# A running log-sum-exp: partition totals in a float32r tile of their own, one-pass matmuls, and the running sum kept in PSUM for three of four chunks

## The chip, the cores and the metric

The kernel runs on one core of a Trainium2 chip. The metric is the device time of one execution in microseconds (us). Every job here timed the kernel before on the same chip in the same rounds. A verdict of faster or slower takes a difference of more than 2%. Ratios are the mean time of one kernel's runs over the mean time of the other's runs of the same rounds, so they are not quite the ratio of the medians quoted beside them.

## The reference

```python
B, S, D = (4, 4096, 4128)                     # x: float32, standard normal
out[:, 0, :] = x[:, 0, :]
for t in range(1, S):                         # logaddexp along S
    mx = np.maximum(out[:, t-1, :], x[:, t, :])
    out[:, t, :] = mx + np.log(np.exp(out[:, t-1, :] - mx) + np.exp(x[:, t, :] - mx))
```

The inputs are small enough to leave the maximum out: the result is the logarithm of a running sum of exponentials along S. 271 MB are read and 271 MB written.

## The kernel before

A step takes 384 rows (256 in four of the 44 steps); each of the 128 partitions holds three (two) consecutive rows of 4128 columns. A step is cut into four chunks of 1024 columns; 32 columns are left over, the tail. Per chunk:

- ScalarE: Exp in place.
- VectorE, `own`: add row 0 to row 1 and row 1 to row 2, so that the last row holds the partition's total.
- TensorE, `head`: a strictly triangular matrix (`excl`) times the totals adds the sum of all partitions above, in PSUM, to the running sum that is there.
- VectorE, `add_above`: add PSUM to all three rows.
- TensorE, `pick`: copy the last row of the last partition, the new running sum, into PSUM for the next step.
- ScalarE: Ln in place; after the fourth chunk the step is stored.

```python
bufs = 4
above = [psum.tile([P, CH], FP32, name=f"above{c}") for c in range(n_main)]   # all of PSUM
above_t = above[last][:, CH - MM:CH - MM + tail]
# ... cut ...
    def own(self):
        x = self.t.xt
        for j in range(1, self.t.r):
            v = x[:, j, self.a:self.b]
            add(v, x[:, j - 1, self.a:self.b], v)
    def head(self):
        for s in range(0, CH, MM):
            mm(above[self.c][:, s:s + MM], excl, t.xt[:, t.r - 1, a + s:a + s + MM],
               start=t.first, stop=True)
    def add_above(self):
        v = t.xt[:, :, a:a + CH]
        add(v, v, above[self.c].unsqueeze(1).to_broadcast([P, t.r, CH]))
    def pick(self, s0=0, s1=CH):
        # ... cut: for each bank
                mm(above[self.c][:, s:s + MM], pick, t.xt[:, t.r - 1, a + s:a + s + MM], start=True)
# ... cut ...
ahead = bufs - 1
for s in steps[:ahead]:
    s.load()
# ... cut: in result(k), after Ln of the last chunk of a step ...
            k.t.store()
            if stored + ahead < len(steps):
                steps[stored + ahead].load()
# ... cut: the order of work, one chunk per turn ...
for g, k in enumerate(chunks):
    chunks[g + 1].own(); chunks[g + 1].head()
    chunks[g + 2].act(ACT.Exp)
    finish(chunks[g - 1]); result(chunks[g - 1])      # tail; Ln, store
    k.add_above(); k.pick()
```

Loads and stores are issued from one queue in this order, and each engine works its instructions in order. Ln of a chunk stands behind Exp of the chunk three places later on ScalarE, and `pick` and `head` read rows that Ln then overwrites.

The softmax here doesn't subtract the row's maximum and nothing guards it: scores larger than these inputs give would overflow.

## Time and profile before

| | before |
|---|---|
| time, median of 3 (range) | 1265.17 us (1264.26 to 1267.58) |
| profiled run | 1268.05 us, span 1266.3 us |
| moved by DMA | 541 MB, 427 GB/s over the span |
| busy: DMA queue / VectorE / ScalarE / TensorE | 99.3% / 77% / 73% / 60% |

The page gives the busy share of each engine, and one line per group of like instructions with what ended the idle time in front of them. "DMA share" in the busy times by stretch is the mean over the 16 DMA engines. The lines themselves stand in the prediction.

One line that it does not show is from the view of who waited for whom in the kernel before (engine and line, waited for: us in total, times, longest us):

```profile
ACT xt L106 <- PE above L74: 33.9, 38, 4.2
```

In 38 of the 44 steps, ScalarE's last Ln waits for matmuls that still read the rows it will overwrite.

### The profile page before, as it was taken

The numbers are of one execution on the slowest core, as the hardware profiler recorded it, in microseconds if no ns is written. First come the engines' busy times: TensorE is split into PE (matmuls) and PEld (weight loads), VectorE is DVE, ScalarE is ACT, GpSimd is POOL, SyncE is SP. The second block draws the span as 40 slices with busy tenths as digits, with TensorE's granted clock in tenths as the row PEclk, the third lists the DMA queues.
The fourth block names the chain that finished last, engine by engine and source line by source line (L and its number), as shares of the span: only waits on it lengthen the run. The fifth ranks groups of instructions, "written<-read, shape, count | busy, mean of one in ns | idle before, by whom it ended". The sixth has DMA issues, their size and how long they took to land.

```text
span 1266.3 us, 4623 instructions
## 1 busy us (share of the span) xinstructions
PE 760.5 (60%) x1512; PEld 289.0 (23%) x1512; DVE 980.6 (77%) x597; ACT 923.8 (73%) x353; POOL 1.1 (0%) x8
## 2 busy tenths in 40 slices
PE   4676665555666666666366666665646656666562
PEld 1222222222222222222122222222212222222220
DVE  3998777777777878788579878777857978787793
ACT  4887666777777777767668777666866877766794
POOL 0000000000000000000000000000000000000000
PEclk9998888887788888888779888888877988888886
DMA  9999999999999999999999999999999999999998
GB/s 409 384 425 424 427 429 443 426 427 440 432 429 441 426 430 440 429 431 433 434 434 434 429 440 430 431 437 433 432 419 434 426 433 433 431 432 438 426 418 349
DMA packets 12695, 541.35 MB, mean 427 GB/s; under 512 B 1409, under 2 KB 1409, under 8 KB 1409
## 3 DMA queue, kind: packets, MB, share of 16 engines
q1 hardware_dynamic: 12672, 541.07, 99.3%
q8 instruction: 12, 0.20, 0.1%
q14 instruction: 11, 0.08, 0.0%
HBM read 270.53 MB, written 270.53 MB: 427 GB/s over the span
## 4 chain that ended last, share of the span: by engine, by line
DMA 67%; DVE 12%; ACT 9%; PE 8%; issue 1%; SPq 0%; ACTq 0%
DMA xt<-in_x_dram 63%; DVE xt L77 12%; ACT xt L106 9%; PE above L74 8%; DMA out_dram<-xt 5%; SPq L97 0%; ACTq L106 0%; SPq L94 0%; DVE carry_t L146 0%
## 5 line engine op out<-in xcount | busy, mean ns | idle before, releaser
L106 ACT ACTIVATE xt<-xt 128x3072 f32<-128x3072 f32 (+2 forms) x352 | 922.5, 2693 | 327.0 <-DMA xt<-in_x_dram 290.5
L74 PE MATMUL above<-xt,excl 128*128 128x512 f32 (+1 forms) x792 | 443.1, 687 | 348.7 <-DVE xt L77 339.4
L77 DVE TENSOR_TENSOR xt<-xt 128x1024 f32<-128x1024 f32 (+1 forms) x336 | 413.4, 1230 | 255.0 <-ACT xt L106 249.4
L77 DVE TENSOR_TENSOR xt<-xt,above 128x3072 f32<-128x3072 f32 (+3 forms) x220 | 582.9, 2651 | 11.7 <-PE above L74 10.3
L74 PE MATMUL above<-xt,pick 128*128 128x512 f32 x640 | 330.7, 630 | 130.0 <-DVE xt L77 130.0
L74 PEld LDWEIGHTS above<-xt,excl 128*128 128x128 f32 x792 | 162.6, 229 | 601.5 <-issue 490.5
L74 PEld LDWEIGHTS above<-xt,pick 128*128 128x128 f32 x640 | 113.6, 198 | 307.4 <-DVE xt L77 227.2
L74 PEld LDWEIGHTS above<-carry_t,pick 128*128 128x128 f32 x80 | 20.8, 271 | 51.4 <-DVE xt L77 48.2
L74 PE MATMUL above<-carry_t,pick 128*128 128x32 f32 x80 | 17.5, 308 | 10.1 <-DVE xt L77 10.1
L146 DVE COPY carry_t<-xt 32x32 f32<-32x32 f32 x40 | 7.1, 178 | 1.4
L56 ACT ACT_TABLE_LOAD x1 | 1.3, 1283 | 0.8 <-PEq L214 0.8
L69 DVE MEMSET carry_t<- 128x32 f32 x1 | 0.1, 85 | 0.9 <-PEq L214 0.9
L27 POOL TENSOR_SCALAR_AFFINE_SELECT pick<-pick 128x128 f32<-128x128 f32 x1 | 0.3, 293 | 0.0
L21 POOL TENSOR_SCALAR_AFFINE_SELECT excl<-excl 128x128 f32<-128x128 f32 x1 | 0.3, 292 | 0.0
L19 POOL MEMSET excl<- 128x128 f32 x1 | 0.2, 204 | 0.3 <-POOLq L214 0.3
L26 POOL MEMSET pick<- 128x128 f32 x1 | 0.2, 204 | 0.0
L214 POOL MEMSET const-bfloat16-1.0<- 128x1 bf16 x1 | 0.1, 101 | 0.0
L214 POOL MEMSET const-uint8-127<- 128x1 uint8 x1 | 0.1, 101 | 0.0
L214 POOL MEMSET const-float32-0.0<- 128x1 f32 x1 | 0.1, 98 | 0.3 <-issue 0.3
L214 POOL MEMSET const-float32-1.0<- 128x1 f32 x1 | 0.1, 98 | 0.0
## 6 DMA issues: line engine op xcount, KB each, us to landing
xt<-in_x_dram SPq DMA_DIRECT2D x40, 6192.0 KB, 41.1
out_dram<-xt SPq DMA_DIRECT2D x40, 6192.0 KB, 27.0
xt<-in_x_dram SPq DMA_DIRECT2D x4, 4128.0 KB, 36.2
out_dram<-xt SPq DMA_DIRECT2D x4, 4128.0 KB, 19.6
```

Of the source, the lines that this page charges most:

```text
L19: nc.gpsimd.memset(excl, 1.0)
L21: nc.gpsimd.affine_select(out=excl, in_=excl, pattern=[[1, P]], compare_op=mybir.AluOpType.is_ge, fill=0.0, base=-1, channel_multiplier=-1,)
L26: nc.gpsimd.memset(pick, 0.0)
L27: nc.gpsimd.affine_select(out=pick, in_=pick, pattern=[[0, P]], compare_op=mybir.AluOpType.not_equal, fill=1.0, base=-(P - 1), channel_mul ...
L56: nc.scalar.preload_act_table_set("natural_log_exp_and_others")
L69: nc.vector.memset(carry_t, 0.0)
L74: nc.tensor.matmul(pt, lhsT=w, rhs=rhs, start=start, stop=stop, skip_group_check=True)
L77: nc.vector.tensor_tensor(out=o, in0=a, in1=b, op=mybir.AluOpType.add)
L106: nc.scalar.activation(v, v, func)
L146: nc.vector.tensor_copy(carry_t[96:, :], t.xt[96:, t.r - 1, t0:D])
L214: nc = _bacc.Bacc("TRN2", target_bir_lowering=False, num_devices=1)
```

## The change

Its intent: a fp32 matmul takes several passes through the array; with the totals in a tile of type float32r it takes one. The tile also frees Ln from waiting for matmuls. The running sum is completed in PSUM by a second triangular matrix, `rest` (`excl` + `rest` = all ones), which the three chunks kept there get in one pass. The last chunk shares its PSUM with the tail, so these two cannot keep their running sum there; they pass it from step to step through a fp32 copy of the last row (`carry`) and a fp32 `pick`. (The aim seems to be that the rounding of float32r does not add up over the steps.) VectorE pays: the last row is now "total tile + PSUM", so the add of three rows becomes one of two rows and one of one row, plus the copy. Three more things came along: four loads are issued at the start instead of three, the last step is no longer pipelined into the one before it, and each step starts with the chunk that has the tail.

```diff
-            for j in range(1, self.t.r):
-                v = x[:, j, self.a:self.b]
-                add(v, x[:, j - 1, self.a:self.b], v)
+            full = tpool.tile([P, CH + tail], FP32R, name="tot")      # two buffers
+            self.tot = full[:, :self.b - self.a]
+            for j in range(1, r - 1):
+                add(self.row(j), self.row(j - 1), self.row(j))
+            add(self.tot, self.row(r - 2), self.row(r - 1))
@@ head
-                mm(above[self.c][:, s:s + MM], excl, t.xt[:, t.r - 1, a + s:a + s + MM], ...)
+                if through:                                            # last chunk
+                    mm(o, pick, carry[:, s:e], start=True)
+                mm(o, excl, self.tot[:, s:e], start=self.t.first)
@@ add_above
-            add(v, v, above[self.c].unsqueeze(1).to_broadcast([P, t.r, CH]))
+                v = t.xt[:, :n, a:b]                                   # n = r - 1
+                add(v, v, p.unsqueeze(1).to_broadcast(v.shape))
+            add(t.xt[:, n, a:b], self.tot[:, a - self.a:b - self.a], p)
+            if cr is not None and not t.final:
+                nc.vector.tensor_copy(cr[96:, :], t.xt[96:, n, a:b])
@@ pick -> complete
+            if self.c != lastc and not self.t.final:
+                for o, s, e in self.banks():
+                    mm(o, rest, self.tot[:, s:e])
@@ loads
-    for s in steps[:ahead]:
+    for s in steps[:bufs]:
         s.load()
-            if stored + ahead < len(steps):
+            if bufs <= stored + ahead < len(steps):
@@ order of work (now starting with the chunk that has the tail)
-    for g, k in enumerate(chunks):
+    for part in (steps[:-1], steps[-1:]):
+        chunks = [Chunk(s, c) for s in part for c in order]
+        for g in range(-2, N + 1):
```

More of the change, by code (lines that the diff above doesn't have):

```diff
@@ L8 @@
 FP32 = mybir.dt.float32
+FP32R = mybir.dt.float32r
 ACT = mybir.ActivationFunctionType
@@ L16, in _constants, with select @@
 def _constants(nc, pool):
-    excl = pool.tile([P, P], FP32, name="excl")
-    nc.gpsimd.memset(excl, 1.0)
-    nc.gpsimd.affine_select(
-        out=excl, in_=excl, pattern=[[1, P]], compare_op=mybir.AluOpType.is_ge,
-        fill=0.0, base=-1, channel_multiplier=-1,
-    )
-    pick = pool.tile([P, P], FP32, name="pick")
-    nc.gpsimd.memset(pick, 0.0)
-    nc.gpsimd.affine_select(
-        out=pick, in_=pick, pattern=[[0, P]], compare_op=mybir.AluOpType.not_equal,
-        fill=1.0, base=-(P - 1), channel_multiplier=1,
-    )
-    return excl, pick
+    def select(dtype, fill, op, base, step, name):
+        t = pool.tile([P, P], dtype, name=name)
+        nc.gpsimd.memset(t.bitcast(FP32), 1.0 - fill)
+        nc.gpsimd.affine_select(
+            out=t, in_=t, pattern=[[step, P]], compare_op=op, fill=fill, base=base,
+            channel_multiplier=-step if step else 1,
+        )
+        return t
+    ge, ne = mybir.AluOpType.is_ge, mybir.AluOpType.not_equal
+    return (
+        select(FP32R, 0.0, ge, -1, 1, "excl"),
+        select(FP32R, 0.0, ge, 0, -1, "rest"),
+        select(FP32, 1.0, ne, 1 - P, 0, "pick"),
+    )
 @with_exitstack
@@ L50, with mm @@
     assert S % P == 0
-    n_main = D // CH
-    tail = D - n_main * CH
-    t0 = n_main * CH
-    last = n_main - 1
+    NC = D // CH
+    tail = D - NC * CH
+    t0 = NC * CH
+    order = [NC - 1] + list(range(NC - 1))
+    firstc, lastc = order[0], order[-1]
     nc.scalar.preload_act_table_set("natural_log_exp_and_others")
     consts = ctx.enter_context(tc.tile_pool(name="consts", bufs=1))
-    excl, pick = _constants(nc, consts)
+    excl, rest, pick = _constants(nc, consts)
     bufs = 4
     xpool = ctx.enter_context(tc.tile_pool(name="xpool", bufs=bufs))
+    tpool = ctx.enter_context(tc.tile_pool(name="tpool", bufs=2))
     cpool = ctx.enter_context(tc.tile_pool(name="cpool", bufs=1))
     psum = ctx.enter_context(tc.tile_pool(name="psum", bufs=1, space=bass.MemoryType.PSUM))
-    above = [psum.tile([P, CH], FP32, name=f"above{c}") for c in range(n_main)]
-    above_t = above[last][:, CH - MM:CH - MM + tail]
+    above = [psum.tile([P, CH], FP32, name=f"above{c}") for c in range(NC)]
+    above_t = above[lastc][:, :tail]
+    carry = cpool.tile([P, CH], FP32, name="carry")
     carry_t = cpool.tile([P, tail], FP32, name="carry_t")
+    nc.vector.memset(carry, 0.0)
     nc.vector.memset(carry_t, 0.0)
     ctx.enter_context(tc.manual_schedule())
-    def mm(pt, w, rhs, start=False, stop=False):
-        nc.tensor.matmul(pt, lhsT=w, rhs=rhs, start=start, stop=stop, skip_group_check=True)
+    def mm(o, w, rhs, start=False):
+        nc.tensor.matmul(o, lhsT=w, rhs=rhs, start=start, stop=True, skip_group_check=True)
     def add(o, a, b):
@@ L101, in __init__, with row @@
             self.t, self.c = step, c
-            self.a, self.b = c * CH, D if c == last else (c + 1) * CH
+            self.a, self.b = c * CH, D if c == NC - 1 else (c + 1) * CH
+        def row(self, j):
+            return self.t.xt[:, j, self.a:self.b]
         def act(self, func):
@@ L108, in own @@
         def own(self):
-            x = self.t.xt
-            for j in range(1, self.t.r):
-                v = x[:, j, self.a:self.b]
-                add(v, x[:, j - 1, self.a:self.b], v)
-        def head(self):
-            t, a = self.t, self.a
-            for s in range(0, CH, MM):
-                mm(above[self.c][:, s:s + MM], excl, t.xt[:, t.r - 1, a + s:a + s + MM],
-                   start=t.first, stop=True)
-        def add_above(self):
-            t, a = self.t, self.a
-            v = t.xt[:, :, a:a + CH]
-            add(v, v, above[self.c].unsqueeze(1).to_broadcast([P, t.r, CH]))
@@ L127, in pick @@
-        def pick(self, s0=0, s1=CH):
-            t, a = self.t, self.a
-            if not t.final:
-                for s in range(s0, s1, MM):
-                    mm(above[self.c][:, s:s + MM], pick, t.xt[:, t.r - 1, a + s:a + s + MM],
-                       start=True)
-        def tail_head(self):
-            t = self.t
-            if not t.first:
-                mm(above_t, pick, carry_t, start=True)
-            mm(above_t, excl, t.xt[:, t.r - 1, t0:D], start=t.first, stop=True)
-        def tail_add(self):
-            t = self.t
-            v = t.xt[:, :, t0:D]
-            add(v, v, above_t.unsqueeze(1).to_broadcast([P, t.r, tail]))
-            if not t.final:
-                nc.vector.tensor_copy(carry_t[96:, :], t.xt[96:, t.r - 1, t0:D])
+            r = self.t.r
@@ new lines, in own, with banks @@
+            full = tpool.tile([P, CH + tail], FP32R, name="tot")
[3 more added lines that the diff above has]
+            add(self.tot, self.row(r - 2), self.row(r - 1))
+        def banks(self):
+            for s in range(0, CH, MM):
+                yield above[self.c][:, s:s + MM], s, s + MM
+        def head(self):
+            through = self.c == lastc and not self.t.first
+            for o, s, e in self.banks():
+                if through:
+                    mm(o, pick, carry[:, s:e], start=True)
+                mm(o, excl, self.tot[:, s:e], start=self.t.first)
@@ new lines, in tail_head, with sums @@
+        def tail_head(self):
+            if not self.t.first:
+                mm(above_t, pick, carry_t, start=True)
+            mm(above_t, excl, self.tot[:, CH:], start=self.t.first)
+        def sums(self, a, b, p, cr):
+            t = self.t
+            n = t.r - 1
+            if n:
+                v = t.xt[:, :n, a:b]
[3 more added lines that the diff above has]
+                nc.vector.tensor_copy(cr[96:, :], t.xt[96:, n, a:b])
@@ L148, with complete @@
+        def add_above(self):
+            self.sums(self.a, self.a + CH, above[self.c], carry if self.c == lastc else None)
+            if self.c == firstc:
+                self.sums(t0, D, above_t, carry_t)
+        def complete(self):
+            if self.c != lastc and not self.t.final:
+                for o, s, e in self.banks():
+                    mm(o, rest, self.tot[:, s:e])
     steps = []
@@ L153 @@
             parts.reverse()
+        assert min(parts) > 1
         row = 0
@@ L158 @@
         assert row == S
-    chunks = [Chunk(s, c) for s in steps for c in range(n_main)]
     ahead = bufs - 1
-    for s in steps[:ahead]:
+    for s in steps[:bufs]:
         s.load()
     stored = 0
-    def finish(k):
-        if k.c == last:
-            k.tail_add()
-            k.pick(CH - MM)
     def result(k):
@@ L172, in result @@
         k.act(ACT.Ln)
-        if k.c == last:
+        if k.c == lastc:
             k.t.store()
-            if stored + ahead < len(steps):
+            if bufs <= stored + ahead < len(steps):
                 steps[stored + ahead].load()
             stored += 1
-    chunks[0].act(ACT.Exp)
-    chunks[1].act(ACT.Exp)
-    chunks[0].own()
-    chunks[0].head()
-    for g, k in enumerate(chunks):
-        if g + 1 < len(chunks):
-            chunks[g + 1].own()
-            chunks[g + 1].head()
-        if g + 2 < len(chunks):
-            chunks[g + 2].act(ACT.Exp)
-        if g:
-            finish(chunks[g - 1])
-            result(chunks[g - 1])
-        k.add_above()
-        if k.c == last:
-            k.tail_head()
-            k.pick(0, CH - MM)
-        else:
-            k.pick()
-    finish(chunks[-1])
-    result(chunks[-1])
+    for part in (steps[:-1], steps[-1:]):
+        chunks = [Chunk(s, c) for s in part for c in order]
+        N = len(chunks)
+        for g in range(-2, N + 1):
+            if 0 <= g + 2 < N:
+                chunks[g + 2].act(ACT.Exp)
+            if 0 <= g + 1 < N:
+                chunks[g + 1].own()
+                chunks[g + 1].head()
+            if 0 <= g < N:
+                chunks[g].add_above()
+                if g + 1 < N and chunks[g + 1].c == firstc:
+                    chunks[g + 1].tail_head()
+                chunks[g].complete()
+            elif g == -1:
+                chunks[0].tail_head()
+            if 0 <= g - 1:
+                result(chunks[g - 1])
 _INS = ['x']
```

## The prediction

> **What bounds the kernel now.** I read the page first, then the busy times by stretch (one row per window), then the timeline at both ends, because the page says that the middle has one owner.
>
> ```profile
> PE 760.5 (60%) x1512; PEld 289.0 (23%) x1512; DVE 980.6 (77%) x597; ACT 923.8 (73%) x353; POOL 1.1 (0%) x8
> ...
> PEclk9998888887788888888779888888877988888886
> DMA  9999999999999999999999999999999999999998
> ...
> q1 hardware_dynamic: 12672, 541.07, 99.3%
> ...
> L74 PE MATMUL above<-xt,excl 128*128 128x512 f32 (+1 forms) x792 | 443.1, 687 | 348.7 <-DVE xt L77 339.4
> L74 PE MATMUL above<-xt,pick 128*128 128x512 f32 x640 | 330.7, 630 | 130.0 <-DVE xt L77 130.0
> ```
>
> No compute engine is above 77%; the DMA queue that carries loads and stores is at 99.3%. The two matmul rows are what the change attacks, but most of the idle time of TensorE in front of them is waiting for VectorE: TensorE is a follower here. The busy times by stretch (columns: window, its length, busy time and number of instructions of PE, PEld, DVE, ACT, POOL, then TensorE clock, DMA share, GB/s) tell where the transfers are not saturated:
>
> ```profile
> 41.00:44.00 3.00, 2.11 (x5) 0.84 (x6) 2.97 (x4) 3.00 (x2) 0.00 (x0) 1.00 0.42 176
> 68.00:70.00 2.00, 1.03 (x3) 0.19 (x1) 2.00 (x1) 2.00 (x2) 0.00 (x0) 1.00 0.94 396
> 100.00:1200.00 1100.00, 666.59 (x1318) 253.00 (x1318) 861.17 (x522) 806.80 (x304) 0.00 (x0) 0.87 1.00 432
> 1234.00:1240.00 6.00, 4.50 (x11) 1.64 (x10) 5.68 (x5) 6.00 (x4) 0.00 (x0) 1.00 0.21 91
> ```
>
> For 1100 us the share is 1.00 at 432 GB/s. The idle time of the transfers is all at the ends: 3 x 0.58 = 1.7 us at 41 us, 2 x 0.06 = 0.1 us at 69 us, 6 x 0.79 = 4.7 us at 1234 us, together 6.5 us, half a per cent of the span. The bytes do not change (541 MB; 541.07 MB at 432 GB/s are 1252 us), so nothing that the change does can win more than these 6.5 us unless the rate itself moves. That decides the verdict; the rest of this text is about the sign of a few microseconds.
>
> **What the Trainium skill says.** (1) "DMA: Bandwidth & Descriptors", Specifications, gives a fabric ceiling of 435 GB/s; the trace agrees, 432 in the long window. So the middle has no reserve. (2) "FP8 and Floating Point Precision", TensorE Precision Notes: true fp32 takes four passes through the array. The trace: an fp32 matmul of 512 columns is two records, which start 0.43 us apart at full clock (the timeline from 23.97 to 25.26 us), so one pass is estimated at 0.21 us. (3) "TensorE: Matmul & The Clock Gate", Part 1: the clock halves when the array idles. The trace agrees: four records take 3.39 us at 1242.92 us, where the granted clock is 0.5. TensorE with less work will be cold more often. (4) "VectorE: DVE Perf Modes", The TRN2 errata: a fp32 tensor_tensor costs (N+151)/0.96 ns. The trace: 128x3072 takes 3348 ns, 128x2048 2282, 128x1024 1222; the formula gives 3357, 2291, 1224. So cutting one add in two costs about 0.15 us.
>
> **The change part by part.** A step is 384 rows (256 in four of the 44), a chunk a quarter of its columns.
>
> *TensorE.* Before, a step has 16 fp32 matmuls of 512 columns (8 excl, 8 pick), 32 records x 0.43 = 13.7 us warm, plus the tail's small ones; the page has 760.5/44 = 17.3 us. After: 8 excl and 6 rest in one pass, 14 x 0.21 = 3.0 us; two fp32 pick matmuls for the last chunk, 4 x 0.43 = 1.7; the tail's 0.6. That is 5.3 us warm, 233 us for 44 steps, and some 300 to 350 us at a colder clock: 410 to 460 us of TensorE work go. All of it lies beside saturated transfers, worth 0 us in the middle.
>
> *VectorE.* The row sums stay (the last goes to the new tile instead of in place). The add from PSUM is cut in two: 2.28 + 1.22 = 3.50 instead of 3.35, four times a step: +0.6 us. The tail's add in two: +0.2. A copy of 32x1024 into the carry: if it runs at two elements a cycle, 0.7 us (estimate from the same page's tier table, fp32 copy 2x). Sum 1.5 us on a step of 23.1 (the row for 1143 to 1172 us shows 23.18 busy in 29): 24.6 us, still below the 29.3 us that two transfers take. Total DVE near 1045 us. Also 0 us in the middle. A wait may appear: with two buffers, the second row sum writes the tile that the rest matmuls of the chunk before are reading, and they start only when the add before has ended; the first row sum (1.2 us) covers two passes, the weight load and a warm clock, about 0.8 us, and just misses a cold one, about 1.4.
>
> *The waits.* Before, the last Ln of a step waits for the matmuls that read its rows in place:
>
> ```profile
> 40.65 20.62 ACT L106 ACTIVATE xt<-xt 128x2112 f32<-128x2112 f32 x8 [1.24 <-PE above L74]
> 65.51 21.50 ACT L106 ACTIVATE xt<-xt 128x3168 f32<-128x3168 f32 x8 [4.25 <-PE above L74]
> ```
>
> With the separate tile nothing on TensorE reads the rows that Ln overwrites, so these go, except through the chain add, copy, Ln.
>
> *Start.* Before, load 3 is issued with store 0, at 43.03 us; the first three loads are moved by 41.3 us and the transfers stand still for 1.7 us. After, four loads are issued at once: 1.6 + 9.8 + 3 x 14.6 = 55.2 us of work (packets of 8 per engine at 1.22 and 1.83 us). Store 0 at about 42 us is in time. Store 1 was issued at 68.38; without the wait for PE I get about 64, working VectorE's queue forward from load 1's landing at 27.7 us at 5.9 us a chunk; store 0 ends at 65. Gain of the start: 1.8 us.
>
> *End.* This is the part that I could get wrong. Before:
>
> ```profile
> 1201.74 13.38 ACT L106 ACTIVATE xt<-xt 128x3072 f32<-128x3072 f32 x5 [7.35 <-DMA xt<-in_x_dram]
> 1215.73 8.23 ACT L106 ACTIVATE xt<-xt 128x3168 f32<-128x3168 f32 x3 [0.61 <-PE above L74]
> 1226.15 20.85 ACT L106 ACTIVATE xt<-xt 128x2048 f32<-128x2048 f32 x10 [2.19 <-DMA xt<-in_x_dram]
> 1249.67 1.96 ACT L106 ACTIVATE xt<-xt 128x2112 f32<-128x2112 f32 x1 [2.67 <-DVE xt L77]
> ```
>
> The last load lands at 1226; the last-but-one store goes out when its Ln is through, at 1240.2 (six activations after 1226.15), 6 us after the transfers ran dry. It takes 14.7 us, to 1254.9, and the last store (ready at 1251.7) follows on its heels for 9.8 us, to 1264.7; 1.6 us later the span ends. After, the last-but-one step is drained alone. From its landing (1201.7 - 1.8 = 1199.9): first row sums done at +5.3, the add and copy of the step before +9.4, row sums +11.7, add with tail +15.8, two chunks of 5.8 to +27.4, last add and copy +31.5, Ln 2.8 to +34.3: store at 1234.2, just as the transfers run dry (1234 - 1.8), so the 4.7 us gap shrinks to 2. But only then does ScalarE, in order, begin the last step. Its chain: Exp 1.95, row sum 1.25, wait for the second Exp, row sum to 5.1, add with tail to 7.8, row sum and add 8.95 and 11.3, 12.5 and 14.9, the last add to 17.4 (perhaps 0.5 more for the two cold fp32 matmuls), Ln 1.95: 19.6 us. Store at about 1254.0, that is 2.3 us later than before. The transfers finished the store before it at 1249 to 1251, so the new gap is some 4 us, and the end is 1254.0 + 0.5 + 9.8 + 1.6 = 1265.9, less than a microsecond below the 1266.3 of before. What separating wins for one store it loses for the next.
>
> *Sum:* start -1.8, end +1.4: about -0.4 us in the span. 1265.17 - 0.4, rounded: 1264.7 us.
>
> **The rivals.** *A: the transfers stay the bound and both ends gain* (the ends' 6.5 us all go, 1259 us). For it: the separate last step clearly aims at it. Against it: the last step then has to be computed in the 15 us that the store before takes, and I count 19.6. *B: VectorE becomes the bound.* 24.6 us a step against 29.3; even with a stall of 0.5 us on three chunks a step it is 26. For it only the copy at one element a cycle (+0.5) and a tile in float32r that adds more slowly, which I see no sign of. If it did reach 30 us a step, 1300 us and more. *C: a serial end.* The drain of both steps longer than counted, stalls of VectorE on cold matmuls (0.5 us a chunk): the span 3 to 4 us longer, 1269 us. *D: transfers hidden anyway, nothing moves*: within 1 us of 1265, which is close to my own number for a different reason.
>
> **Range and chances.** The start is worth 0 to -2, the end -5 to +4, and the three runs of before lie 3.3 us apart. So 1260 to 1269 us. Both edges are inside 2% (1240 to 1290), and only B or a changed rate leaves it: within 2% 0.97, faster 0.01, slower 0.02.
>
> **What would show it.** Right: DMA share 1.00 at 432 GB/s in the long window; PE busy falls to 300 or 350 us and the clock with it; DVE rises to about 1045 us; ScalarE no longer waits for PE before Ln; the gap at 41 us is gone; the last-but-one store is issued about 34 us after its load landed and the last one about 20 us after that, with transfers idle for some 4 us between. Wrong: DVE busy above 1150 us or long waits of DVE for PE (B); idle transfers in the middle; a last store issued before 1251 us (A). The prediction fails if VectorE's ops on the new type have another cost than the fp32 ones, or if the rate of the transfers changes with the order of loads and stores.

## The result, and the profile after

The changed kernel takes 1265.7 us (median of 4, 1264.33 to 1265.97), the kernel before 1264.72 us in the same rounds: ratio 1.0003, 95% interval 0.9984 to 1.0021. A second comparison, 5 runs against 9, is E12 below: 1.0004 (0.9992 to 1.0017). The result is correct, and the change moves nothing.

The page of the changed kernel: busy totals, TensorE clock and DMA in 40 slices, the DMA queue, and the three groups of matmuls.

```profile
PE 480.5 (38%) x876; PEld 220.3 (17%) x876; DVE 1024.4 (81%) x858; ACT 921.0 (73%) x353; POOL 1.5 (0%) x10
...
PEclk9865555565555555556556565656555656555656
DMA  9999999999999999999999999999999999999997
...
q1 hardware_dynamic: 12672, 541.07, 99.4%
...
L83 PE MATMUL above<-tot,excl 128*128 128x512 f32 (+1 forms) x396 | 255.1, 714 | 476.9 <-DVE tot L86 472.6
...
L83 PE MATMUL above<-tot,rest 128*128 128x512 f32 x240 | 129.2, 633 | 205.1 <-DVE xt L86 205.1
L83 PE MATMUL above<-carry,pick 128*128 128x512 f32 x160 | 139.5, 972 | 0.0
```

TensorE has 280 us less to do and its granted clock fell from 0.87 to 0.58; VectorE has 44 us more; the DMA queue is as full as it was. The stretches of the changed kernel, in the columns of the prediction:

```profile
41.00:44.00 3.00, 1.22 (x2) 0.50 (x2) 2.83 (x6) 3.00 (x3) 0.00 (x0) 1.00 1.22 528
100.00:1200.00 1100.00, 423.48 (x769) 193.27 (x768) 901.22 (x749) 803.71 (x306) 0.00 (x0) 0.56 1.00 433
1228.00:1233.00 5.00, 0.00 (x0) 0.00 (x0) 0.87 (x2) 4.00 (x2) 0.00 (x0) 0.50 0.67 287
1247.00:1252.00 5.00, 0.00 (x0) 0.00 (x0) 1.57 (x2) 3.23 (x2) 0.00 (x0) 0.87 0.27 116
```

(A packet counts in the stretch where it starts, so a short one can show more than 1.) The idle stretch at 41 us is gone. The one at 1234 us has become two: 5 x 0.33 = 1.7 us in front of the last store but one, 5 x 0.73 = 3.7 us in front of the last. ScalarE at the end, from its timeline:

```profile
1197.23 21.50 ACT L118 ACTIVATE xt<-xt 128x3168 f32<-128x3168 f32 x8 [7.74 <-DMA xt<-in_x_dram]
1219.08 2.76 ACT L118 ACTIVATE xt<-xt 128x3072 f32<-128x3072 f32 x1 [0.34 <-DVE xt L86]
1224.94 2.77 ACT L118 ACTIVATE xt<-xt 128x3072 f32<-128x3072 f32 x1 [3.10 <-DVE xt L86]
1229.00 10.02 ACT L118 ACTIVATE xt<-xt 128x3072 f32<-128x3072 f32 x5 [1.29 <-DVE carry L155]
...
1248.67 1.91 ACT L118 ACTIVATE xt<-xt 128x2048 f32<-128x2048 f32 x1 [0.35 <-DVE xt L86]
```

The load of the last step but one lands at 1197.2. Its last Ln is the first 2.8 us of the group at 1229.00; it ends at 1231.8, and the first Exp of the last step follows at once. The very last Ln ends at 1250.6. So the lone last step takes 18.8 us, while the store before it is moved in 14.6 (8 packets of 1.83 us on each engine).

### The profile page after: what moved, and what is told of

It reads as the page before. It is cut to its first block, busy times and chain, and to the rows that moved or that the text cites. A ratio compares the mean times of both kernels' runs of the same rounds, so it can differ in the third digit from the quotient of the medians.

```text
span 1262.5 us, 3545 instructions
## 1 busy us (share of the span) xinstructions
PE 480.5 (38%) x876; PEld 220.3 (17%) x876; DVE 1024.4 (81%) x858; ACT 921.0 (73%) x353; POOL 1.5 (0%) x10
## 3 DMA queue, kind: packets, MB, share of 16 engines
q1 hardware_dynamic: 12672, 541.07, 99.4%
## 4 chain that ended last, share of the span: by engine, by line
DMA 69%; ACT 19%; issue 7%; DVE 3%; SPq 0%; PE 0%; DVEq 0%; ACTq 0%
DMA xt<-in_x_dram 63%; ACT xt L118 19%; DMA out_dram<-xt 6%; DVE xt L86 3%; DVE tot L86 1%; SPq L106 0%; PE above L83 0%; DVE carry L155 0%; DVEq L239 0%; ACTq L118 0%; DVE carry_t L155 0%; DVEq L86 0%
## 5 line engine op out<-in xcount | busy, mean ns | idle before, releaser
L118 ACT ACTIVATE xt<-xt 128x3072 f32<-128x3072 f32 (+3 forms) x352 | 919.7, 2692 | 328.8 <-DMA xt<-in_x_dram 315.0
L83 PE MATMUL above<-tot,excl 128*128 128x512 f32 (+1 forms) x396 | 255.1, 714 | 476.9 <-DVE tot L86 472.6
L86 DVE TENSOR_TENSOR xt<-xt,above 128x2048 f32<-128x2048 f32 (+3 forms) x220 | 393.4, 1788 | 0.0
L86 DVE TENSOR_TENSOR xt<-xt 128x1024 f32<-128x1024 f32 (+1 forms) x160 | 197.0, 1231 | 179.9 <-ACT xt L118 177.5
L86 DVE TENSOR_TENSOR tot<-xt 128x1024 fp32r<-128x1024 f32 (+1 forms) x176 | 217.1, 1234 | 40.4 <-ACT xt L118 18.9
L86 DVE TENSOR_TENSOR xt<-tot,above 128x1024 f32<-128x1024 f32 (+1 forms) x220 | 221.5, 1007 | 0.0
L83 PEld LDWEIGHTS above<-tot,excl 128*128 128x128 f32 x396 | 104.4, 305 | 607.4 <-DVE tot L86 566.9
L83 PE MATMUL above<-tot,rest 128*128 128x512 f32 x240 | 129.2, 633 | 205.1 <-DVE xt L86 205.1
L83 PE MATMUL above<-carry,pick 128*128 128x512 f32 x160 | 139.5, 972 | 0.0
L83 PEld LDWEIGHTS above<-tot,rest 128*128 128x128 f32 x240 | 53.1, 276 | 295.9 <-DVE xt L86 294.1
```

Of the source, the lines that this page charges most:

```text
L83: nc.tensor.matmul(o, lhsT=w, rhs=rhs, start=start, stop=True, skip_group_check=True)
L86: nc.vector.tensor_tensor(out=o, in0=a, in1=b, op=mybir.AluOpType.add)
L118: nc.scalar.activation(v, v, func)
```

## The experiments

My theory: the DMA engines are the bound in the middle, nothing on the compute engines counts there, and only the two ends could move. The main rivals: the one-pass matmuls do pay and VectorE gives it back; or the gain waits at the ends and is lost to the order of work there.

### E1: transfers alone

All arithmetic taken out of the changed kernel; each store waits for its load. Wrong result.

```diff
-                chunks[g + 2].act(ACT.Exp)
-                chunks[g + 1].own(); chunks[g + 1].head()
-                chunks[g].add_above() ...
-        k.act(ACT.Ln)
```

> The changed kernel with all arithmetic taken out (no Exp, sums, matmuls or Ln): the same 44 loads and 44 stores, each store waiting for its load alone. The result is wrong on purpose. My theory (the transfers are the bound, about 433 GB/s, and all else lies beside them): a span of about 1257 us, the sum of the packets' time (1254.7 us in the profile of before) plus 1.6 us before and after; time 1258 to 1261 us, 0.4% below both kernels. Rival (the compute holds the transfers back in the middle, or slows their packets): clearly faster, under 1240 us, with packets shorter than 1.83 us.

Measured: 1258.34 us against 1264.17 (ratio 0.9951, 0.9938 to 0.9965), as expected. (The 1254.7 us in the expectation is close to the packet time of the changed kernel, 99.4% of 1262.5; the profile of before has 99.3% of 1266.3, 1257.4 us.) Three stretches of this run (columns: window, length, DVE, ACT and POOL busy, clock, DMA share, GB/s):

```profile
100.00:1200.00 1100.00, 0.00 (x0) 0.00 (x0) 0.00 (x0) 1.00 1.00 433
1250.00:1253.00 3.00, 0.00 (x0) 0.00 (x0) 0.00 (x0) 1.00 0.61 264
1253.00:1255.00 2.00, 0.00 (x0) 0.00 (x0) 0.00 (x0) 1.00 0.15 66
```

Without a single instruction of compute the middle runs at 433 GB/s, the rate of both kernels. That settles the middle: compute takes next to nothing from it. The last two lines held a warning that I passed over at first. There is nothing to wait for at the end of this run, and yet the share falls to 0.15 (two to three of the 16 DMA engines, on the mean) before the end: the engines do not finish together.

### E2: the kernel before, with four loads at the start

```diff
-    for s in steps[:ahead]:
+    for s in steps[:bufs]:
-            if stored + ahead < len(steps):
+            if bufs <= stored + ahead < len(steps):
```

> The kernel before with one part of the change: four loads at the start instead of three. Theory: the idle stretch of the transfers at 41 us goes (1.7 us), the end is as before: 1.5 to 2 us less, a ratio to before of about 0.9985. Rival (what is won at the start is waited for again later, because the end is set by another wait): ratio 1.000, with a longer idle stretch near 1234 us.

Measured: 1264.71 against 1264.17 us, ratio 1.0000 (0.9988 to 1.0013). The 1.7 us did not come; the rival's number is right. Its place for them was not quite: the stretch at 41 us is full, and the transfers run dry later, at 66 us, because the second store is not there yet. E10, which starts the same way, shows it at its worst. ScalarE's timelines of E2 and then of E10:

```profile
63.80 13.54 ACT L106 ACTIVATE xt<-xt 128x3168 f32<-128x3168 f32 x5 [2.55 <-PE above L74]
```

```profile
66.58 13.54 ACT L106 ACTIVATE xt<-xt 128x3168 f32<-128x3168 f32 x5 [5.19 <-PE above L74]
```

and the transfers of E10 behind it:

```profile
66.00:70.00 4.00, 4.00 (x9) 1.48 (x7) 4.00 (x2) 3.42 (x2) 0.00 (x0) 0.86 0.14 58
```

The second store hangs on that Ln, which waits 2.55 us or 5.19 us for TensorE; the store is issued at about 66.7 us in E2 and 69.5 in E10. By the packet records, four loads and the first store are done by 67.4 us in E2 and 67.8 in E10. In the changed kernel Ln does not wait for TensorE, the second store is issued at 63.8 us, and the transfers do not run dry. So the early load alone does not fill the start, Ln has to be free of TensorE as well; and E4 will show that the tile of its own is not enough either if its matmuls are slow. One thing stays open: in E2's own profiled run the late store costs only some 0.5 us, so the profile leaves 1 us or more of gain that the median of five runs does not show.

### E3: the changed kernel, with the end pipelined again

```diff
-    for part in (steps[:-1], steps[-1:]):
+    for part in (steps,):
```

> The changed kernel with its end undone: the last step is pipelined into the one before, as in the kernel before. Theory: the idle time at the end only moves back from between the last two stores to in front of the last but one; two gaps of 2.3 and 3.9 us become one of 4 to 6 us: span 1261 to 1264 us, the same as the changed kernel within 2 us. Rival A (separating the last step is worth its 4.7 us): 4 us slower than the changed kernel. Rival B (it costs): 3 us faster.

Measured: 1263.66 us, ratio to before 0.9993 (0.9980 to 1.0005), where the changed kernel has 1.0003 and 1.0004. The profile has one idle stretch at the end, 10 x 0.66 = 6.6 us from 1226 to 1236 us, and none in front of the last store. As the theory said, separating the last step only moves the idle time; it may cost 1 us, which these intervals do not resolve (the packet records, below E12, show 0.8).

### E4: the changed kernel, with its matmuls in fp32

```diff
-FP32R = mybir.dt.float32r
+FP32R = mybir.dt.float32
```

> The changed kernel with the new tile and its two constants in fp32 instead of float32r, so that its matmuls take four passes again: the part that the change is named for, undone alone. Theory (TensorE lies beside the transfers): the same as the changed kernel within 3 us, PE busy back above 750 us, VectorE waiting for TensorE in front of the row sum that writes the tile (0.5 to 1 us a chunk, 60 to 130 us in all against 11), hidden in the middle; only the end is longer by 1 to 3 us. Rival (the one-pass matmuls do pay, and the split adds of VectorE give it back): 1% or more slower than the changed kernel.

Measured: 1273.38 us, ratio to before 1.0070 (1.0057 to 1.0082). Neither expectation holds: more than my 3 us, less than the rival's 1%. Where the 8 us come from is in the waits and stretches. First the changed kernel's wait of VectorE for TensorE, then the same in E4 with three stretches of E4:

```profile
DVE tot L86 <- PE above L83: 11.4, 43, 1.4
```

```profile
DVE tot L86 <- PE above L83: 92.5, 92, 2.1
```

```profile
66.00:72.00 6.00, 2.19 (x6) 1.36 (x7) 5.90 (x6) 4.04 (x2) 0.00 (x0) 0.73 0.38 160
1233.00:1240.00 7.00, 0.59 (x2) 0.00 (x0) 2.57 (x3) 5.71 (x3) 0.00 (x0) 0.73 0.59 255
1253.00:1261.00 8.00, 2.84 (x6) 1.06 (x6) 4.57 (x4) 4.45 (x3) 0.00 (x0) 0.94 0.04 19
```

The row sum that writes the tile waits for the four-pass `rest` matmuls that read it. In the middle that is hidden. At the start the second store is late and the transfers stand for 6 x 0.62 = 3.7 us; at the end for 7 x 0.41 + 8 x 0.96 = 10.6 us, where the changed kernel has 1.7 + 3.7 = 5.4. Together 8.9 us, against some 8 us measured (0.67% of 1264). So within this arrangement the one-pass matmuls are worth about 8 us, all of it at the ends, and they pay for what the rest of the change costs there.

### E5 and E6: the compute without its transfers

The compute of both kernels on all columns, with loads and stores of only the first 1024 after the first four (full) loads. The result is wrong.

```diff
+    held = [xpool.tile([P, R, D], FP32, name=f"xt{i}") for i in range(bufs)]
-            nc.sync.dma_start(out=self.xt, in_=self.dram(x))
+            nc.sync.dma_start(out=self.xt[:, :, :CH], in_=self.dram(x)[:, :, :CH])   # first four: whole tile
-            nc.sync.dma_start(out=self.dram(out), in_=self.xt)
+            nc.sync.dma_start(out=self.dram(out)[:, :, :CH], in_=self.xt[:, :, :CH])
-            nc.scalar.activation(v, v, func)
+            nc.scalar.activation(v, v, func, scale=0.125 if func == ACT.Exp else 1.0)
```

> The kernel before with a quarter of the transfers: four full tiles are loaded once, then each step loads and stores only its first 1024 columns and computes on all; Exp has a scale of 0.125, so that the recycled values stay in range. The result is wrong on purpose. It shows how fast the compute alone goes. Theory: VectorE sets the pace, 24 to 25 us a step as in the profile of before between 43 and 93 us (stores 25.7 and 24.2 us apart), so 1070 to 1110 us. Rival (TensorE sets it): the same time, but with VectorE idle more than 15% of the middle, waiting for PE or for Ln that waits for PE.

> The changed kernel with the same quarter of the transfers (wrong on purpose as well). Theory: what the matmuls no longer cost, the split adds and the copy of the carry do cost on VectorE, so the compute alone is no faster either: 24.5 to 25.5 us a step, 1080 to 1125 us, a ratio to the run before it of 1.00 to 1.02. Rival (the change does pay, and only the transfers hide it): at least 3% faster than the kernel before with a quarter of the transfers.

Measured: 1043.44 us for the kernel before, 1079.0 us for the changed one: the change makes the compute 3.4% slower (1079.0/1043.44). The theory's numbers missed: the kernel before is quicker than I had read off its start (1070 to 1110 us), so the ratio of the two is 1.034 and not 1.00 to 1.02. The rival for E6, a change that pays once most of the transfers are gone, has the wrong sign. The busy totals, E5 and then E6:

```profile
PE 727.6 (70%) x1512; PEld 271.7 (26%) x1512; DVE 977.1 (94%) x597; ACT 919.7 (88%) x353; POOL 1.1 (0%) x8
```

```profile
PE 474.8 (44%) x876; PEld 217.6 (20%) x876; DVE 1021.3 (95%) x858; ACT 932.6 (87%) x353; POOL 1.5 (0%) x10
```

VectorE is the bound of the compute in both, at 94 and 95%. TensorE, at 70% in E5, was not it. The 44 us that the change adds to VectorE show up nearly whole, as 36 us.

### E7 and E8: more work for VectorE

Small adds of 128x100 on VectorE, three or six per chunk, in 37 steps of the middle of the changed kernel.

```diff
+            if steps[4].row_id <= self.t.row_id < steps[-3].row_id:
+                for _ in range(3):                                     # E8: 6
+                    add(dummy, pick[:, :100], pick[:, :100])
```

> The changed kernel with three small adds (128x100, about 0.28 us each) more per chunk on VectorE, in the steps from the fifth to the last but three: 3.4 us more a step, so some 28.0 of the 29.3 us that two transfers take. Theory (slack in the middle): the time stays within 3 us of the changed kernel, DVE busy about 1150 us. Rival (VectorE is already nearly the bound, and the time between add and Ln matters): 20 us or more longer.

> The same with six small adds: 6.7 us more a step, so some 31.3 us on VectorE against 29.3 us of transfers in 37 steps. Theory: the bound passes to VectorE, (31.3 - 29.3) x 37 = 74 us longer, less the slack of the first of these steps: 1310 to 1345 us, with idle transfers in the middle. Rival (more slack than counted): under 1290 us.

Measured: 1267.62 us with three (ratio to before 1.0028), 1331.1 us with six (1.0530), both as the theory said, the first at the edge of its 3 us. In E8 the long stretch has lost its full DMA share:

```profile
100.00:1200.00 1100.00, 402.96 (x717) 183.46 (x716) 1053.79 (x1557) 772.10 (x289) 0.00 (x0) 0.55 0.97 410
```

By the busy totals the adds were 2.8 and 5.8 us a step (1127.3 and 1240.8 against 1024.4 us, over 37 steps). The first dose cost 2 to 3 us in the whole kernel, the second 63 us or 1.7 us a step: the changed kernel has some 4 us of slack a step on VectorE. (The small loss of E7 is not waiting: in its profile a packet of a full row takes 1840 ns on the mean, against 1836 in the changed kernel, 2.5 us over the 640 that each engine moves. Whether the adds slow the packets, no run separates from the differences between runs.)

### E9 and E10: the end filled with smaller stores

The last two steps are stored chunk by chunk, in the changed kernel (E9) and in the kernel before with four loads (E10).

```diff
         k.act(ACT.Ln)
+        parts = k.t in steps[-2:]
+        if parts:
+            k.t.store(k.a, k.b)            # this chunk's columns only
```

> The changed kernel, whose last two steps are stored chunk by chunk, each chunk as soon as its Ln is done, instead of in two whole stores. Theory (what is left above the transfers alone is the idle stretch in front of the last two stores): both stretches go, span 1256 to 1258 us, time 1258 to 1260 us, a ratio to before of 0.995 to 0.9965, within 1.5 us of the run with transfers alone. Rival (the last stores wait for something else, or smaller pieces move more slowly): 1262 us or more.

> The kernel before with four loads at the start and the same stores by chunk in the last two steps, its fp32 matmuls and its in-place sums untouched. Theory: the matmuls do not matter for the end either, once the pieces are small: 1258 to 1261 us, within 1.5 us of the changed kernel with the same stores. Rival (the one-pass matmuls or the lone last step are needed to fill the end): 3 us or more above it.

Measured: 1264.14 us (ratio to before 1.0002, 0.9988 to 1.0015) and 1265.27 us (1.0012, 0.9999 to 1.0024). This was to be the version that beats both, and the theory fell: 1258 to 1260 was expected. The stretches of E9 at its end:

```profile
1232.00:1253.00 21.00, 7.41 (x15) 3.71 (x15) 14.18 (x14) 13.84 (x8) 0.00 (x0) 0.66 1.02 412
1253.00:1256.00 3.00, 0.00 (x0) 0.00 (x0) 0.00 (x0) 0.00 (x0) 0.00 (x0) 0.50 0.69 279
1256.00:1258.00 2.00, 0.00 (x0) 0.00 (x0) 0.00 (x0) 0.00 (x0) 0.00 (x0) 0.50 0.17 68
1258.00:1261.00 3.00, 0.00 (x0) 0.00 (x0) 0.00 (x0) 0.00 (x0) 0.00 (x0) 0.50 0.06 26
```

The idle stretches are filled, as intended: share 1.02 up to 1253 us. All compute has ended by then. But from there on the DMA engines drop out one after the other: on the mean of the stretch, three of 16 are at work from 1256 us (0.17 x 16) and one from 1258 us (0.06 x 16); the last packet ends at 1260.3. The kernel ends when the slowest DMA engine has moved its part. Filling the stretches won nothing, and the records offer two reasons. One is that the rival is partly right: the small pieces move more slowly, 412 GB/s at a share of 1.02 where whole rows reach 433 at 1.00. By the packet records the pieces took 26.0 us of each engine; the same bytes at the rate of whole rows are an estimated 24.5. The other is that the slowest engine had little idle time in the stretches to begin with. The idle time that I had added up, here and in the prediction, belongs for the most part to the engines that run ahead: they wait for the next store while the laggard is still busy with the last one. The packet records, at the end of this section, show it.

### E11 and E12: both kernels again, unchanged

> The kernel before, unchanged, as a control and for a second profile: the profiled run that I predicted from took 1268 us, the longest of all its runs. Ratio 1.000 within 0.0012. If four loads at the start are worth nothing because the profiled run was unusual, the idle stretch of the transfers at 41 us is absent or under 0.5 us here; if it is there again (about 2 us), then the run with four loads gave the 2 us back in slower packets, which is noise between runs.

> The changed kernel, unchanged, on the same chip and in the same rounds as the other three, to narrow its interval and to see its two idle stretches at the end again (2.3 and 3.9 us). Ratio to before 0.9985 to 1.0010.

Measured: 1263.82 us (1.0004) and 1264.69 us (1.0004), each against the 9 other runs of the kernel before, 1263.93. The stretches of E11 and then of E12:

```profile
41.00:44.00 3.00, 2.11 (x5) 0.83 (x6) 2.97 (x4) 3.00 (x2) 0.00 (x0) 1.00 0.42 176
...
1230.00:1236.00 6.00, 4.48 (x10) 1.44 (x8) 5.93 (x5) 6.00 (x4) 0.00 (x0) 1.00 0.25 107
```

```profile
1228.00:1233.00 5.00, 0.00 (x0) 0.00 (x0) 0.96 (x2) 3.91 (x2) 0.00 (x0) 0.50 0.60 258
1247.00:1252.00 5.00, 0.00 (x0) 0.00 (x0) 1.67 (x2) 3.32 (x2) 0.00 (x0) 0.91 0.27 116
```

The stretch at 41 us is a property of the kernel before (0.42 again), not of one run; so the run that I predicted from was long, but not for that reason. Idle on average: before 3 x 0.58 + 6 x 0.75 = 6.2 us, after 5 x 0.40 + 5 x 0.73 = 5.7 us. The spans are 1262.1 and 1262.7 us: the mean idle time went down by half a microsecond and the span up by as much. A sum over a mean of 16 engines is not exact to a microsecond, which is all that is at stake here.

The packet records of the traces, which hold when each packet starts and how long it takes, say more than the mean. The time in which no data packet at all is in flight:

| run | at the start, us | at the end, us |
|---|---|---|
| before, E11 | 1.50, 1.47 | 0.24, 0.13 |
| changed kernel, E12 | 0, 0 | 1.06, 1.06 |
| E2 (before, four loads) | 0.07 | 0.12 |
| E3 (changed, end pipelined) | 0 | 0.28 |
| E4 (changed, fp32) | 3.93 | 5.10 |
| E9 (changed, smaller stores) | 0 | 0 |
| E10 (before, four loads, smaller stores) | 2.54 | 0 |

So of the 4.7 us of mean idle time at the end of the kernel before, only 0.24 us are a standstill. Its stretches of 1 us show the same, and after them two of the changed kernel:

```profile
1238.00:1239.00 1.00, 0.71 (x2) 0.47 (x3) 1.00 (x2) 1.00 (x1) 0.00 (x0) 1.00 0.11 50
1239.00:1240.00 1.00, 1.00 (x3) 0.20 (x2) 1.00 (x1) 1.00 (x2) 0.00 (x0) 1.00 0.00 0
```

```profile
1249.00:1250.00 1.00, 0.00 (x0) 0.00 (x0) 0.00 (x0) 1.00 (x1) 0.00 (x0) 1.00 0.00 0
1250.00:1251.00 1.00, 0.00 (x0) 0.00 (x0) 0.00 (x0) 0.57 (x1) 0.00 (x0) 0.83 0.00 0
```

50 GB/s for 1 us are 50 KB, one packet of a full row (49.5 KB). It is the laggard's last, and it is in flight until 1240.35; the next store's first packets start at 1240.58. In the changed kernel the laggard ends at 1250.38, and the last store, issued at 1250.60, has its first packets at 1251.44. The change wins a standstill of 1.5 us at the start and pays 0.8 to 0.9 us at the end. E3 gives 0.8 us back, and E4 stands still for 8.0 us more than the changed kernel, which is its loss. What is left between E11 and E12 can lie in the packets: a full row took 1835.9 ns on the mean in E12 and 1834.6 in E11, which is 0.8 us over 640.

## Why the prediction was right

The range and the verdict were right, for the reason given: the transfers are the bound in the middle (share 1.00 at 433 GB/s with and without compute, E1), VectorE has slack there (E7), and so has TensorE (E4: four passes cost nothing in the middle), and the two ends nearly cancel. That the number, 1264.7 us, came within 1 us is luck as well: the gain of 0.4 us that it forecast is less than the runs resolve (-1.0 to +2.1 us in E12, with a mean on the other side of zero), and the time alone cannot tell it from rival D, nothing moves. What speaks against D is the profile, in which both ends did move. By its own steps:

- **Middle, 0 us.** Right. E1 shows it, and E8 shows where it would stop.
- **TensorE, 300 to 350 us.** Mis-sized: 480.5 us. The one pass is what I took it for: at half clock a single matmul of 512 columns takes 0.79 us and a pair 1.22, so one more costs 0.43. But I took 1.3 to 1.5 times the warm 233 us for the cold clock, and the array now idles so much that it is granted 0.58 on average and 730 of the 876 matmul records start at half clock (308 of 1512 before), with what a lone matmul or pair costs on top: 2.1 times. It costs nothing, because it lies beside transfers.
- **VectorE, about 1045 us.** 1024.4. The pieces were right: the copy of 32x1024 takes 691 ns, the two adds 2280 and 1214 ns. But neighbours overlap by some 0.08 us, and there are more of them: the durations of the changed kernel add up to 40 us more than its busy time, those of before to 23.
- **The new wait for the tile's buffer.** There, and small: 11.4 us in 43 waits. E4 shows what it would be with four passes.
- **Start, -1.8 us.** The standstill of 1.5 us is gone, and the stores are where I put them (41.3 and 63.8 us; 42 and 64 predicted). E2 shows that the early load alone is not enough, a point that the prediction made only in passing, and E4 that it takes the one-pass matmuls too, a point that it did not make.
- **End, +1.4 us.** The mechanism is right: last-but-one store 34.5 us after its load landed (34.3 predicted), the last one 18.8 us later (19.6), 3.7 us idle between (some 4). The net is of the size predicted: in mean idle time 5.7 against 4.5 us (E12 and E11), +1.2 us; in standstill +0.8 to +0.9; in time, E3 puts it at about 1, inside its interval. The sum had a small error: from the issue of a store to its first packets I took 0.5 us, and it is 0.84.
- **Rival A, the 6.5 us of the ends can be won.** Here an argument failed. I took the 6.5 us for the most that the change could win, and rejected A only for lack of time in the last step. They are a mean over 16 engines, and the slowest one was hardly waiting: before, the standstill is 1.7 us in all. E9 and E10 filled the stretches at the end and won nothing. One sign that I had named for A, a last store issued before 1251 us, did come (1250.6), but not for A's reason: everything in this run lies earlier than I had assumed (the load landed at 1197.2, not 1199.9). The Trainium skill has the words for it: "Perfetto Trace Analysis", What "DMA-bound" means, lists "Specific DMA engines" first. The trace agrees: 0.06 of 16 engines is one engine, the mean of the last 3 us of E9.
- **Rivals B and C** did not come. B needed a slower add on the new type; `tot` as output takes 1225 ns, the fp32 add beside it 1223.

What stays open: why the slowest engine ends later with compute (1260.3 us in E9) than without (1255.1 us in E1), at the same rate in the middle. The small pieces of E9 are not the whole reason: without them the changed kernel ends its last packet at 1261.4 us, which less its standstill is 1260.3 too. The page of the changed kernel counts 20 packets of instructions fetched by the same DMA engines, E1's counts two; and I count more data packets that took over 1.9 us instead of 1.83 (140 in E9, 124 in the changed kernel, 82 in E1, from the packet records). Both go in the right direction; no run separates them, and the records do not name the engine.

## What to carry to other kernels

When a DMA queue is at 99% and a run without any arithmetic is within half a per cent of the kernel, relieving a compute engine is worth nothing in the middle, even if it takes a third of that engine's work; what it can win or lose lies at the ends (8 us in E4). Look first at which engine would be next (here VectorE, where the change cost 3.4% of the compute). Idle DMA time averaged over 16 engines is no reserve: count the time in which none of them is at work, and how many are in the last microseconds, because the slowest one sets the end. Smaller stores that fill a gap can cost in rate what they win in time. And an earlier load pays only if the store that comes after it is no longer waiting for something else.

## What the Trainium skill lacked or had wrong

- "DMA: Bandwidth & Descriptors" (Specifications) gives one rate per engine and a ceiling for all 16. The runs reach 433 GB/s in the middle, close to it, but no page says by how much the 16 engines part over a millisecond: in E1, with transfers alone, the share is down to 0.61 from 1250 to 1253 us and 0.15 from 1253 to 1255; in E9 the last engine ends at 1260.3 us, when the share has been below 0.2 for 4 us.
- "FP8 and Floating Point Precision" (TensorE Precision Notes) counts four passes for true fp32 and says that a reduced form exists, but gives no cost for it. Here a float32r matmul of 512 columns takes one pass: 0.43 us for each further one at half clock (a pair takes 1.22 us, a single one 0.79), and one record each (240 for the 240 `rest` matmuls), where the fp32 `pick` of the same width has two (160 for 80).
- "VectorE: DVE Perf Modes" (The TRN2 errata) has a table whose PSUM→SBUF entry for VectorE costs about 60 cycles more than its SBUF→SBUF entry. The adds here, with one input in each, cost no more: 1214 ns for 128x1024 with PSUM as the second input, 1222 ns with both in SBUF. The page's own formula for a fp32 tensor_tensor, and the two-elements-a-cycle copy (691 ns for 1024 columns), hold.
